# Queuing the leftover work of a decoder layer behind the tile ahead, issuing stores from ScalarE, and transposing new keys into two kinds of PSUM banks

## The chip, the cores and the metric

The kernel runs on one core of a Trainium2 chip. The metric is the device time of one execution in microseconds (us), lower is better.

## What is computed

One inference step of one hybrid decoder layer, for a prompt of 2048 tokens and for 64 new tokens (8 sequences of 8) that look back into a cache of keys and values:

```python
h = rms_norm(x, g_norm)
proj = jnp.einsum('bsd,de->bse', h, w_in)            # 1024 -> 3584 columns
u, va, za, q, k, vb, zb = jnp.split(proj, SPLITS, axis=-1)
...
# mixer A: chunked spatial gating, 4 groups of 128 channels
mixed = jnp.einsum('gts,bnsgc->bntgc', ws, vc) + b_s
a = rms_norm(u * mixed) * jax.nn.silu(z)
...
# mixer B: 8 heads of 64, three dilated windows (128,1), (512,4), (2048,16)
s = jnp.einsum('brnqhd,brnkhd->brnhqk', qb, kb) * SCALE
...
o = jnp.einsum('brnhqk,brnkhd->brnhqd', p, vb) / den
b = combine_by_denominator(outs, lses)
...
h = x + jnp.einsum('bse,ed->bsd', jnp.concatenate([a_out, b], axis=-1), w_out)
gate = jax.nn.sigmoid(jnp.einsum('bsd,de->bse', h, w_ple_gate))
e = rms_norm(jnp.einsum('bsp,pd->bsd', p, w_ple), g_ple)
return h + gate * e
```

The same steps are done for the new tokens, whose attention reads the cached keys and values (2048 rows for each of 8 sequences) beside the new ones.

## The kernel before

The prompt is cut into 16 tiles of 128 rows; the 64 new tokens are a 17th tile of half the height. The input projection has eight chunks of weights, four for mixer A (384 columns) and four for mixer B (512 columns), taken in the order A0, B0, B1, A1, B2, B3, A2, A3. In each chunk the loop runs over the 17 tiles: `gemm` (L473) makes 24 matmuls into a PSUM tile `psg`, for a chunk of A ScalarE and VectorE gate the result (L613 to L617, tanh and multiply, the last reader of the PSUM bank is the multiplication into `agz`), and 4 tiles make one group for the spatial mixing (L648 to L671). The new tokens' rows are split over both halves of the partitions and folded together (`fold`, L483 to L487, with one DMA between).

Between the projection's matmuls a pump lays the dilated attention of the chunks already done. A unit of it is: scores on TensorE (L823, PSUM `pss`), mask and maximum on VectorE (L829), exp on ScalarE (L838), its high half (L841), the low half on VectorE (L842), a transposing DMA on SP's queue (`pT`<-`pc`, L763), the product with the values on TensorE (L869 to L871, PSUM `pso`), and its eviction on ScalarE (`rec`, L875), which a DMA stores to one of the scratch tensors `r1d`, `r2d`, `r3d` (L883). There are 160 such `pc` tiles and 96 such stores. When the three windows of a pair of heads are done, `combine` loads them back (L891), joins them (L901 to L926) and stores the result to `catd` (L928). Four groups of rows are joined for each pair of heads.

The last part takes the tiles one after the other: `p3_cat` loads a row tile of `catd`, splits it into two fp16 halves and transposes them by DMA (`halves_T`, L995 to L998, tile `Tc`), `p3_out` multiplies by `w_out` (gemm2, L1008, 48 matmuls) and adds the residual (L1055), `p3_gate` does the same with `Th`, `p3_ple` with `Tp` (12 matmuls). Its weights are prepared during the last chunk: load (L940), squares (L949), scale and split (L964 on ScalarE, L965 on VectorE). Among these matmuls stands the new tokens' attention, `sample(hp)` for each of the four head pairs: a step for each block of cached keys transposes it on TensorE (L1243, four transposes into PSUM `pst`), copies it to SBUF on ScalarE (`KT`, L1253), and multiplies (L1248); a second part multiplies the keys by the queries on GpSimd (L1263) and sums them on VectorE (L1264).

Each engine's instructions run in the order of its queue. That order is set when the program is built, by a scheduler that sorts by the order of writing and its own reckoning of when each operand is there. `tc.issue_after(ins)` puts the instructions of a block, on the engine of `ins`, behind `ins`. DMAs are issued by the queue of SP throughout, apart from a few small ones on GpSimd.

## Time and profile before

| | before |
|---|---|
| time, median of 3 executions (lowest, highest) | 1474.05 us (1469.55, 1478.37) |
| the profiled execution | 1471.11 us, of which the span 1469.4 us |
| TensorE (PE) busy | 1296.9 us, 88% |
| VectorE (DVE) busy | 999.6 us, 68% |
| ScalarE (ACT) busy | 821.8 us, 56% |
| GpSimd (POOL) busy | 315.7 us, 21% |
| mean granted clock of TensorE | 0.954 |

The span is the time from the first to the last instruction. TensorE is idle for 1469.4 − 1296.9 = 172.5 us of it, and the profile tells for each of these waits which line waited and what ended it. The granted clock is the share of TensorE's full clock that the chip gave in a stretch.

### The profile page before, as it was taken

What the parts mean: (1) busy time and instruction counts of PE and PEld (TensorE: products, weight loads), DVE (VectorE), ACT (ScalarE), POOL (GpSimd) and SP (SyncE); (2) the same over time, 40 slices, a digit from 0 to 9 for tenths busy, and PEclk for the clock granted to TensorE, in tenths of its full rate; (3) what the DMA queues carried; (4) which work ended last, traced back from release to release, by engine and by line L of the source; (5) the groups of instructions that cost most, each with busy time, mean ns of one, the idle gap of its engine ahead of it and who ended that gap; (6) DMA issues with size and microseconds to landing.
All of it is one profiled execution on the core that took longest, in us unless ns stands there. A gap on an engine that the chain in (4) does not pass through costs nothing.

```text
span 1469.4 us, 26262 instructions
## 1 busy us (share of the span) xinstructions
PE 1296.9 (88%) x8600; PEld 674.0 (46%) x8600; DVE 999.6 (68%) x3018; ACT 821.8 (56%) x2269; POOL 315.7 (21%) x279
## 2 busy tenths in 40 slices
PE   4899998998898897899788985569998998999998
PEld 2564454544564554455455653224443443444343
DVE  4675776777777698777778788885455456456364
ACT  5785778966679677687677884553222122123122
POOL 8221001102101111100120025311152143134001
PEclk9899999999999999999999998779999999999999
DMA  5954598799847989978996798976899799989542
GB/s 145 235 132 114 124 173 182 173 222 226 193 112 165 206 188 209 178 185 189 222 213 145 154 247 216 288 173 170 203 210 245 181 203 229 230 184 231 137 88 65
DMA packets 589592, 271.32 MB, mean 185 GB/s; under 512 B 323184, under 2 KB 571056, under 8 KB 589456
## 3 DMA queue, kind: packets, MB, share of 16 engines
q1 hardware_dynamic: 587472, 268.00, 80.7%
q0 software_dynamic: 1984, 1.66, 0.7%
q8 instruction: 67, 1.10, 0.3%
q14 instruction: 69, 0.57, 0.1%
HBM read 136.94 MB, written 55.08 MB: 131 GB/s over the span
## 4 chain that ended last, share of the span: by engine, by line
PE 44%; DMA 23%; DVE 14%; ACT 11%; issue 4%; SPq 3%; POOL 1%; DVEq 0%; ACTq 0%; POOLq 0%
PE psg L473 14%; PE psg L1008 11%; PE pss L1008 10%; DMA pT<-pc 6%; DMA rl<-r2d 2%; DVE sm L829 2%; ACT sm L838 2%; DMA K<-in_cache_k_dram 2%; DMA qB<-qd 2%; DMA wst<-in_w_in_dram 2%; PE pso L1343 2%; DVE pc L842 2%; PE pso L1248 2%; ACT kc L715 1%; DMA rl<-r3d 1%
## 5 line engine op out<-in xcount | busy, mean ns | idle before, releaser
L473 PE MATMUL psg<-wt,xT 128*128 128x512 f16 (+1 forms) x3072 | 640.6, 363 | 31.3 <-DVE agz L617 26.5
L473 PEld LDWEIGHTS <-xT 128*128 128x128 f16 x3072 | 301.7, 100 | 299.7 <-issue 44.3
L193 POOL TENSOR_TENSOR sm<-sm,mhalf 128x1 f32<-128x1 f32 (+5 forms) x115 | 145.6, 1271 | 790.4 <-DVE sm L532 324.6
L838 ACT ACTIVATE sm<-sm,rec 128x256 f32<-128x256 f32 (+1 forms) x384 | 151.7, 459 | 38.9 <-DVE rec L834 35.8
L829 DVE CUSTOM_DVE_ANT_0 sm<-pss,mask,psc 128x256 f32<-128x256 f32 (+1 forms) x384 | 145.1, 419 | 12.2 <-PE pss L823 8.5
L1008 PEld LDWEIGHTS <-Tc 128*128 128x128 f16 x800 | 76.8, 99 | 116.0 <-issue 28.5
L1263 POOL TENSOR_TENSOR K<-K,qB 96x512 f32<-96x512 f32 x64 | 94.1, 1475 | 161.2 <-DMA qB<-qd 62.3
L842 DVE TENSOR_TENSOR pc<-sm,pc 128x512 f16<-128x512 f32 (+1 forms) x160 | 104.2, 653 | 34.1 <-ACT pc L841 32.7
L1008 PEld LDWEIGHTS <-Th 128*128 128x128 f16 x800 | 76.7, 98 | 109.0 <-issue 15.3
L995 ACT ACTIVATE hl<-x,sm 128x1024 f16<-128x1024 f32 (+1 forms) x17 | 19.5, 1148 | 147.3 <-DVE sm L976 132.4
L869 PEld LDWEIGHTS <-pT 128*128 128x128 f16 x600 | 57.1, 98 | 96.1 <-DMA pT<-pc 90.5
L1008 PE MATMUL psg<-w,Th 128*128 128x512 f16 x400 | 95.8, 381 | 5.0 <-DMA Th<-hl 5.0
L841 ACT ACTIVATE pc<-sm 128x512 f16<-128x512 f32 (+1 forms) x160 | 96.0, 603 | 7.2 <-DMA pT<-pc 6.2
L1008 PE MATMUL psg<-w,Tc 128*128 128x512 f16 x400 | 97.0, 386 | 2.8 <-DMA Tc<-hl 2.8
L1264 DVE TENSOR_REDUCE blk<-K 96x8 f32<-96x512 f32 x64 | 43.4, 680 | 79.5 <-POOL K L1263 79.5
L1008 PE MATMUL pss<-w,Tc 128*128 128x512 f16 x400 | 96.0, 382 | 0.0
L1008 PE MATMUL pss<-w,Th 128*128 128x512 f16 x400 | 93.4, 379 | 0.0
L823 PEld LDWEIGHTS <-qk 128*128 128x128 f16 x960 | 74.2, 120 | 29.3 <-issue 5.9
L1100 POOL TENSOR_TENSOR tg<-tg,x 128x1024 f32<-128x1024 f32 (+1 forms) x16 | 37.6, 2348 | 153.9 <-DVE tg L1099 141.8
L869 PE MATMUL pso<-v,pT 128*128 128x65 f16 x248 | 32.2, 201 | 42.4 <-DMA pT<-pc 42.4
L869 PE MATMUL pso<-vt,pT 128*128 128x65 f16 x352 | 43.5, 195 | 28.9 <-DMA pT<-pc 28.8
L715 ACT ACTIVATE kc<-qk 128x512 f16<-128x512 f16 x72 | 58.9, 872 | 13.8 <-DMA qk<-qkd 8.5
(321 smaller groups left out, 2239.5 us busy)
## 6 DMA issues: line engine op xcount, KB each, us to landing
qB<-qd SPq DMA_DIRECT2D x64, 192.0 KB
K<-in_cache_k_dram SPq DMA_DIRECT2D x64, 192.0 KB
V<-in_cache_v_dram SPq DMA_DIRECT2D x64, 192.0 KB
vt<-vscr SPq DMA_DIRECT2D x32, 258.0 KB
K<-in_cache_k_dram SPq DMA_DIRECT2D x32, 256.0 KB
cat<-catd SPq DMA_DIRECT2D x16, 512.0 KB
x<-in_x_prompt_dram SPq DMA_DIRECT2D x16, 512.0 KB
V<-in_cache_v_dram SPq DMA_DIRECT2D x32, 256.0 KB
```

What stands on the lines that cost most here:

```text
L193: nc.gpsimd.tensor_tensor(y, src, mhalf[:p, :n], op=ALU.pow)
L473: last_mm[0] = nc.tensor.matmul(g[:, :ncol], lhsT=l, rhs=r, start=(n == 0), stop=(n == (23 if j < NT else 15)))
L715: nc.scalar.activation(t[:, h], src[:, h], AF.Copy)
L823: nc.tensor.matmul(pss[:, s, h, b * w:(b + 1) * w], lhsT=Q[:, h, qs], rhs=keys(h, k), start=(i == 0 and b == 0), stop=(i == 1 and b == n - 1))
L829: nc.vector.tensor_tensor_reduce(sm4[:, s, h], pss[:, s, h], mk, psc, -3.0e38, op0=ALU.add, op1=ALU.max, accum_out=mx[:, i:i + 1])
L838: nc.scalar.activation(sm4[:, s, h], sm4[:, s, h], AF.Exp, bias=r[:, sl + s, h, HD + 1:HD + 2])
L841: nc.scalar.activation(pc[:, :n], smv, AF.Copy)
L842: nc.vector.tensor_tensor(pc[:, n:2 * n], smv, pc[:, :n], op=ALU.subtract)
L869: nc.tensor.matmul(po[:, q, h, 0:65], lhsT=H, rhs=v[:, vs_, a:a + 65], start=(bi == 0), stop=False)
L1008: last_mm[0] = nc.tensor.matmul(gs[hf], lhsT=o[part][:, kt], rhs=w[:, kt % 2, half, :], start=(n[hf] == 0), stop=(n[hf] == (3 if m == P el ...
L1263: nc.gpsimd.tensor_tensor(K3, K3, qB, op=ALU.mult)
L1264: nc.vector.tensor_reduce(s3[:, b, :, ts_].rearrange("p h t -> p t h"), K3.rearrange("p t (h d) -> p t h d", d=HD), axis=AX.X, op=ALU.add)
```

## The change

It has four parts.

1. A helper `late()` puts a block's instructions behind the last projection matmul on TensorE, and behind the last marked instruction on three other queues: on VectorE the last full tile's gating multiplication (L617, L526) or residual addition (L1055), on ScalarE the last gating tanh (L616, L525, L1096), on SP the last transposing DMA (L763, or the second one of `halves_T`, L998). The blocks are `combine`, every step of the preparation of the last part's weights, and every step of `sample`.
2. ScalarE's queue issues the 96 stores of `rec` (L883), the 14 moves of the fold (L484), and half of the first chunk's eight weight loads (L351): 114 DMAs that SP issued before.
3. The transposes of the new tokens' cached keys go by turns to PSUM tag "o" (two buffers) and "t" (one buffer); before, all went to "t".
4. In the last chunk the new tokens' tile is projected after the eighth tile; before, it came last.

```diff
+    last_on = {}
+    def late():
+        c = ExitStack()
+        for i in [last_mm[0]] + list(last_on.values()):
+            if i is not None:
+                c.enter_context(tc.issue_after(i.ins))
+        return c
...
-                    nc.sync.dma_start(t[:, k2, :ncol].rearrange("p (s c) -> p s c", c=P), src)
+                    (nc.scalar if fast and k2 else nc.sync).dma_start(
+                        t[:, k2, :ncol].rearrange("p (s c) -> p s c", c=P), src)
...
-        nc.sync.dma_start(c[:TS, :n], c[TS:, :n])
+        nc.scalar.dma_start(c[:TS, :n], c[TS:, :n])
...
-        nc.scalar.activation(th[:m], g[:m, 256:384], AF.Tanh, scale=sc[:m, 2:3])
-        nc.vector.scalar_tensor_tensor(G["gz"][:m, q, :], th[:m], 1.0, g[:m, 256:384], op0=ALU.add, op1=ALU.mult)
+        tanh = nc.scalar.activation(th[:m], g[:m, 256:384], AF.Tanh, scale=sc[:m, 2:3])
+        gate = nc.vector.scalar_tensor_tensor(G["gz"][:m, q, :], th[:m], 1.0, g[:m, 256:384], op0=ALU.add, op1=ALU.mult)
+        if m == P:
+            last_on.update(dve=gate, act=tanh)
...
-                nc.sync.dma_start(o["pT"][:, :2 * o["n"] // P, :], o["pc"][:, :2 * o["n"]], transpose=True)
+                last_on["sp"] = nc.sync.dma_start(o["pT"][:, :2 * o["n"] // P, :], o["pc"][:, :2 * o["n"]], transpose=True)
...
-                combine(hp, jg, sc, *got)
+                with late():
+                    combine(hp, jg, sc, *got)
...
-            nc.sync.dma_start(dst[:, s0:s0 + 2], rc)
+            nc.scalar.dma_start(dst[:, s0:s0 + 2], rc)
...
-            nc.vector.scalar_tensor_tensor(h[:m, sl], gs[hf][:m], cm[:m], h[:m, sl], op0=ALU.mult, op1=ALU.add)
+            last_on["dve"] = nc.vector.scalar_tensor_tensor(h[:m, sl], gs[hf][:m], cm[:m], h[:m, sl], op0=ALU.mult, op1=ALU.add)
...
-                pt = pst("t", 1)
+                pt = pst(*(("o", 2) if n % 2 else ("t", 1)))
...
-            yield from sample(hp)
+            steps = sample(hp)
+            while True:
+                with late():
+                    dt = next(steps, None)
...
-        for j in range(NT + 1):
+        for j in range(NT + 1) if ci + 1 < len(order) else [*range(8), NT, *range(8, NT)]:
...
-                    next(nxt, None)
+                    with late():
+                        next(nxt, None)
```

How the change moves instructions is seen at three places. The first is VectorE's queue at the last gating multiplications of the last chunk (L617 before, L629 after; `agz` is their result). Before, one of them stands behind this run, in which `w` is a prepared weight tile (L965), `blk` a sum of the new tokens' scores (L1264) and `gzl` a joined group (L926):

```order
2254 L965 SCALAR_TENSOR_TENSOR w_2247_12774<-w3st_12344,sm_12701,w_2247_12774 128x512
2255 L1264 TENSOR_REDUCE blk<-K_2448_13668 96x4x2
2256 L965 SCALAR_TENSOR_TENSOR w_2247_12774<-w3st_12344,sm_12701,w_2247_12774 128x512
2257 L926 TENSOR_TENSOR gzl_12559<-rl_12553,gzl_12559 128x512
2258 L965 SCALAR_TENSOR_TENSOR w_2250_12809<-w3st_12346,sm_12701,w_2250_12809 128x512
2259 L667 TENSOR_SCALAR sm_12755<-sm_12755,sm_10973 128x4
2260 L965 SCALAR_TENSOR_TENSOR w_2250_12809<-w3st_12346,sm_12701,w_2250_12809 128x512
2261 L965 SCALAR_TENSOR_TENSOR w_2251_12814<-w3st_12348,sm_12701,w_2251_12814 128x512 x2
2262 L624 TENSOR_SCALAR sm_12824<-sm_12543,sm_10973 128x4
2263 L617 SCALAR_TENSOR_TENSOR agz_12545<-th_12821,psg_12784 128x128
```

After, the last full tile's gating multiplication stands among the new tokens' small masks and the last attention unit, ahead of the joining (`rl`, L917 to L936):

```order
2237 L1200 CAST sc_12952<-blk 128x64
2238 L857 TENSOR_TENSOR pc_12405<-sm_12390,pc_12405 128x512
2239 L1201 SCALAR_TENSOR_TENSOR blk<-sc_12952,blk 128x64
2240 L638 TENSOR_SCALAR sm_13191<-sm_12904,sm_10973 128x4
2241 L629 SCALAR_TENSOR_TENSOR agz_12906<-th_13188,psg_13115 128x128
2242 L681 TENSOR_SCALAR sm_13131<-sm_13131,sm_10973 128x4
2243 L1202 TENSOR_SCALAR blk<-blk 128x64
2244 L1206 CAST sc_12952<-blk 128x16
2245 L917 TENSOR_TENSOR sm_12663<-sm_12663,rl_12554 128x8
```

The tiles of `w_out` and of the gate weights (`w` at L980 in the changed kernel) stand behind this point, from row 2270 on, and no sum L1264 stands ahead of them.

The second place is TensorE's queue where the last part begins (`Tc`, the first joined tile). Before, the product of the new tokens' `Tp` with its weights stands directly ahead of it:

```order
12302 L1008 LDWEIGHTS Tp_12991
12303 L1008 MATMUL psg_13216<-w_2132_12170,Tp_12991 128x512
12304 L1008 LDWEIGHTS Tp_12991
12305 L1008 MATMUL psg_13216<-w_2132_12170,Tp_12991 128x512
12306 L1008 LDWEIGHTS Tc_13122
12307 L1008 MATMUL pss_13288<-w_2238_12708,Tc_13122 128x512
```

After, the last attention units' products with the values (L884 to L886, before L869 to L871) stand there, and a sum over partitions of the weights' squares (L283):

```order
12302 L885 LDWEIGHTS pT_12574
12303 L885 MATMUL pso_12576<-vt_12230,pT_12574 128x64
12304 L886 LDWEIGHTS pT_12574
12305 L886 MATMUL pso_12576<-vt_12230,pT_12574 128x65
12306 L283 MATMUL pso_12729<-sm_12632,ones 128x1
12307 L1023 LDWEIGHTS Tc_13180
12308 L1023 MATMUL psg_13274<-w_2245_12740,Tc_13180 128x512
```

Before, the attention's last product stood 137 projection matmuls of the prompt ahead of the end of the projection; after, the last four units' products stand behind all of them.

The third place is the stores of the attention's results. Before, they stand in SP's queue among the transposing DMAs (`pT`<-`pc`):

```order
340 L883 DMA r2d_112<-rec_6647 128x264
341 L763 DMA_TRANSPOSE pT_6985<-pc_6876 128x8x128
342 L763 DMA_TRANSPOSE pT_7188<-pc_7041 128x4x128
343 L556 DMA out_dram<-vo_6822 128x4x128
344 L557 DMA vscr_101<-v_1189_6821 128x4x258
345 L558 DMA zscr_105<-gz_6823 128x4x128
346 L763 DMA_TRANSPOSE pT_7205<-pc_7056 128x8x128
347 L686 DMA vt_7740<-vscr_101 128x1032
348 L883 DMA r2d_112<-rec_6709 128x264
```

After, such a store stands in ScalarE's queue directly behind the eviction (L890) that fills it, ahead of the next unit's exp (L853) and high half (L856):

```order
837 L531 ACTIVATE v_1292_7332<-psg_7529 128x2x64
838 L890 ACTIVATE rec_7062<-pso_7400 128x4x65
839 L898 DMA r1d_109<-rec_7062 128x2x132
840 L853 ACTIVATE sm_7262<-sm_7262,rec_7209 128x128 x2
841 L401 ACTIVATE wt_7646<-wst_6430,sm_7147 128x512 x2
842 L856 ACTIVATE pc_7273<-sm_7262 128x256
```

SP's queue loses 114 DMAs (1187 to 1073 instructions) and ScalarE's gains them.

## Rows read from the trace of the kernel before

**Rows 1.** The page's first part: each engine's busy time, share of the span, instructions.

```profile
PE 1296.9 (88%) x8600; PEld 674.0 (46%) x8600; DVE 999.6 (68%) x3018; ACT 821.8 (56%) x2269; POOL 315.7 (21%) x279
```

**Rows 2.** TensorE's waits: tile and line, what ended them, us in total, times, longest.

```profile
PE pso L869 <- DMA pT<-pc: 71.2, 57, 3.4
PE psg L473 <- DVE agz L617: 26.5, 3, 15.0
PE pst L1243 <- ACT KT L1253: 19.6, 6, 6.6
PE pso L274 <- DVE junk L304: 16.9, 1, 16.9
```

**Rows 3.** Busy time by stretch: PE, PEld, DVE, ACT, POOL; PE's clock; DMA share; GB/s.

```profile
400.00:600.00 200.00, 180.10 (x1448) 102.65 (x1447) 159.66 (x577) 153.36 (x440) 30.10 (x20) 0.96 0.82 177
880.00:940.00 60.00, 33.75 (x189) 18.70 (x190) 50.58 (x98) 25.01 (x77) 27.95 (x20) 0.80 0.95 238
940.00:1000.00 60.00, 43.40 (x180) 18.31 (x179) 53.77 (x139) 35.51 (x87) 13.10 (x11) 0.83 0.85 205
1000.00:1100.00 100.00, 99.51 (x521) 43.27 (x520) 50.92 (x108) 25.44 (x59) 24.98 (x18) 1.00 0.80 195
```

**Rows 4.** Timeline of TensorE, 880 to 945: start, us, line, tiles [wait, its end].

```profile
883.02 12.84 PE L473 MATMUL psg<-wt,xT 128*128 128x384 f16 x78
...
912.13 5.70 PE L473 MATMUL psg<-wt,xT 128*128 128x384 f16 x24 [14.97 <-DVE agz L617]
929.03 0.80 PE L473 MATMUL psg<-wt,xT 128*128 128x384 f16 x2 [11.21 <-DVE agz L617]
...
939.18 2.75 PE L1008 MATMUL pss<-w,Tc 128*128 128x512 f16 x12
```

**Rows 5.** VectorE's groups from 889 to 912 by line: count, busy us, mean ns.

```profile
L965 DVE SCALAR_TENSOR_TENSOR w<-w3st,sm,w 128x512 f16<-128x512 f32 x15 | 11.6, 805 | 0.0
L1264 DVE TENSOR_REDUCE blk<-K 96x8 f32<-96x512 f32 x6 | 4.1, 679 | 1.4 <-POOL K L1263 1.3
...
L617 DVE SCALAR_TENSOR_TENSOR agz<-th,psg 128x128 f32<-128x128 f32 x2 | 0.5, 274 | 0.0
```

**Rows 6.** Timelines of VectorE, SP and ScalarE from a joined group to `Tc`.

```profile
908.28 0.68 DVE L926 TENSOR_TENSOR gzl<-rl,gzl 128x512 f32<-128x512 f32 x1
908.99 1.10 SPq L928 DMA_DIRECT2D catd<-gzl  x1
918.07 0.46 SPq L1031 DMA_DIRECT2D cat<-catd  x1
929.81 1.20 ACT L995 ACTIVATE hl<-cat,sm 128x1024 f16<-128x1024 f32 x1
931.04 2.99 SPq L996 DMA_TRANSPOSE Tc<-hl  x1
...
995.61 0.74 DVE L965 SCALAR_TENSOR_TENSOR w<-w3st,sm,w 128x512 f16<-128x512 f32 x1
```

**Rows 7.** Timelines of TensorE, ScalarE and VectorE at one wait for a copy.

```profile
1124.71 1.12 PE L1243 MATMUL pst<-ident,K 128*128 128x128 f32 x4 [4.83 <-ACT KT L1253]
...
1121.59 1.15 ACT L995 ACTIVATE hl<-x,sm 128x1024 f16<-128x1024 f32 x1 [12.61 <-DVE sm L976]
...
1116.20 0.68 DVE L1264 TENSOR_REDUCE blk<-K 96x8 f32<-96x512 f32 x1 [7.53 <-POOL K L1263]
```

**Rows 8.** SP's queue, its waits: us in total, times, longest.

```profile
SPq L763 <- DVE pc L842: 59.5, 39, 6.0
...
SPq L883 <- ACT rec L875: 21.4, 21, 2.8
```

**Rows 9.** The stores at L883 into one scratch tensor: ns min/median/max, first and last start.

```profile
L883 SPq DMA_DIRECT2D r2d<-rec x32: 319/500/988, 182.5 to 881.6; - x32
```

**Rows 10.** Timelines of SP and ScalarE at the start, the first chunk's weights.

```profile
1.93 6.45 SPq L351 DMA_DIRECT2D wst<-in_w_in_dram  x8
...
11.98 0.61 ACT L367 ACTIVATE junk<-wst,gno 128x384 bf16<-128x384 f32 x1 [4.58 <-DMA wst<-in_w_in_dram]
```

More of the change, by code (lines that the diff above doesn't have):

```diff
@@ L524, in b_evac @@
         th = wk.tile([P, P], F32, name=nm("th"), tag="th", bufs=2)
-        nc.scalar.activation(th[:m], g[:m, 384:512], AF.Tanh, scale=sc[:m, 2:3])
-        nc.vector.scalar_tensor_tensor(G["gz"][:m, q, :], th[:m], 1.0, g[:m, 384:512], op0=ALU.add, op1=ALU.mult)
+        tanh = nc.scalar.activation(th[:m], g[:m, 384:512], AF.Tanh, scale=sc[:m, 2:3])
+        gate = nc.vector.scalar_tensor_tensor(G["gz"][:m, q, :], th[:m], 1.0, g[:m, 384:512], op0=ALU.add, op1=ALU.mult)
+        if m == P:
+            last_on.update(dve=gate, act=tanh)
     def b_norm(G, sc, gch):
@@ L615, in a_evac @@
         th = wk.tile([P, P], F32, name=nm("th"), tag="th", bufs=2)
-        nc.scalar.activation(th[:m], g[:m, 256:384], AF.Tanh, scale=sc[:m, 2:3])
-        nc.vector.scalar_tensor_tensor(G["gz"][:m, q, :], th[:m], 1.0, g[:m, 256:384], op0=ALU.add, op1=ALU.mult)
+        tanh = nc.scalar.activation(th[:m], g[:m, 256:384], AF.Tanh, scale=sc[:m, 2:3])
+        gate = nc.vector.scalar_tensor_tensor(G["gz"][:m, q, :], th[:m], 1.0, g[:m, 256:384], op0=ALU.add, op1=ALU.mult)
+        if m == P:
+            last_on.update(dve=gate, act=tanh)
     def a_norm(G, sc, gch):
@@ L997, in halves_T @@
         nc.vector.scalar_tensor_tensor(lo[:m], t[:m], r[:m], hi[:m], op0=ALU.mult, op1=ALU.subtract)
-        nc.sync.dma_start(dst[1], lo[:m], transpose=True)
+        last_on["sp"] = nc.sync.dma_start(dst[1], lo[:m], transpose=True)
         return o, mx, r
@@ L1095, in p3_gate @@
             sl = slice(hf * 512, hf * 512 + 512)
-            nc.scalar.activation(t[:m, sl], gs[hf][:m], AF.Tanh, scale=cm[:m])
+            last_on["act"] = nc.scalar.activation(t[:m, sl], gs[hf][:m], AF.Tanh, scale=cm[:m])
         dst = yp[j * P:(j + 1) * P] if j < NT else ysm
@@ L1372, in all_samples @@
         for hp in range(4):
-            yield from sample(hp)
+            steps = sample(hp)
+            while True:
+                with late():
+                    dt = next(steps, None)
+                if dt is None:
+                    break
+                yield dt
     ring = dict(cat=[], x=[])
@@ L1474, in tile_hymba_gmlp_dilated_attn_step @@
                 for _ in range(1 if ci else FIRST_PREP[j]):
-                    next(nxt, None)
+                    with late():
+                        next(nxt, None)
             else:
                 for _ in range(LAST_PREP[j]):
-                    if next(nxt, None):
-                        break
+                    with late():
+                        if next(nxt, None):
+                            break
                 if j == 12:
@@ L1541, in tile_hymba_gmlp_dilated_attn_step, with deal @@
     last, cur, samp = None, 0, True
+    def deal():
+        with late():
+            next(nxt, None)
     for k in range(23):
-        pump.later(850.0 * (k + 1), lambda: next(nxt, None))
+        pump.later(850.0 * (k + 1), deal)
     p3_ple(0)
```

## The prediction

> **What bounds the kernel now.** I read the busy times first [rows 1]: TensorE works for 1296.9 us of a span of 1469.4, VectorE for 999.6, ScalarE for 821.8. The change adds and removes no matmul, so its gain can only come out of TensorE's 172.5 idle us, or out of matmuls that ran at a reduced clock. Next come the waits of TensorE [rows 2]. Four entries make 134.2 us of the 172.5: the attention's products wait for the transposed weights `pT` (71.2 us in 57 waits, 1.2 us on the mean), the projection waits for VectorE's gating multiplication to free a PSUM bank (26.5 us in 3 waits), the transposes of the new tokens' keys wait for ScalarE's copy (19.6 us in 6), and the start waits once for 16.9 us. Third come the stretches [rows 3]: in the attention stage (400 to 600 stands for it) TensorE is busy for 180 us in 200, with VectorE at 160 and ScalarE at 153 close below; at the turn from projection to the last part, 880 to 1000, it works for 33.8 + 43.4 = 77.2 us in 120, at a granted clock of 0.80 and 0.83; from 1000 on it is all but full. So the turn is the dear place, and there the order of VectorE's queue decides: TensorE's two long waits of 14.97 and 11.21 us end with a gating multiplication [rows 4], and between two of these stand 15 weight preparations of 805 ns and 6 sums of 679 ns, 15.7 us of VectorE's time, with hardly any idle time in front of them [rows 5].
>
> The sum is made against the profiled execution, 1471.1 us (span 1469.4 and 1.7 outside). The median of the runs shown is 1474.05, so I subtract the same difference from that. About 0.5% (7.4 us) is what a measurement of this kernel can tell from no change.
>
> **A. The start.** SP takes 6.45 us to issue the eight weight loads, and ScalarE waits until 11.98 for one of them [rows 10]. With half of the issues on ScalarE's queue, which has nothing else to do then, the last is issued up to 3.2 us sooner and the next input tile with it. Above: 3.2, and a little more from the tile, 5 us. Below: if the loads are limited by their transfers, nothing, or a loss of 1 because the loads now compete with the first input tile. The wait ends 3.6 us after SP's last issue, so transfers count as much as issues; I take 2. By the Trainium skill, page "DMA: Bandwidth & Descriptors", section "Issuing engines are not separate DMA queues", DMAs of all issuing engines run on the same 16 DMA engines, and spreading them saves only the time to initiate them, usually small; if no issue time lies on the path, this term is 0 and the sum 2 us higher.
>
> **B. The attention stage, up to 880.** 96 stores and the fold's moves go from SP to ScalarE. One costs SP 0.5 us (the median of the 32 into one tensor [rows 9]), so about 110 × 0.45 to 0.5 = 50 to 55 us leave SP, and with the stores goes SP's waiting at its head for `rec`, 21.4 us [rows 8]. This matters where a `pT` transposition stands behind such a store. But SP waits 59.5 us for `pc` itself [rows 8]: most transpositions are late because VectorE is, not because SP is, and that is untouched. On the other side, no row shows a DMA issue on ScalarE. Bounds: nothing, or SP's 0.5 us each, in front of an exp or a high half that lead to the next `pc`. ScalarE is busy for 77% of the stretch [rows 3], so there are some 45 us of 200 free, and some 12 us of issues in each 200 fit. Combine and preparation behind the tile's gating free VectorE for the gates in these chunks, too. If all of SP's relief reached TensorE's waits, 30 us of the 71.2 would go; if all of the issues stood in the path of the 57 waits, 57 × 0.5 = 28 us would come. Between these ends I take a gain of 4: the row it is nearest to is SP's 21.4, of which a fifth lies ahead of a transposition that TensorE waits for.
>
> **C. The turn, 880 to 1000.** The two long waits, 26.2 us, are VectorE's queue order, and this order is what the change moves: the weights' preparation and the sums stand behind the last gate instead of between the gates. What stays between two gates (masks, groups' gating, attention) is work of some 1 to 10 us, an estimate from the new order and durations like those in [rows 5], against 4 us for a tile's 24 matmuls (12.84 / 78 each [rows 4]), so some waits of a few us stay. Also 24 matmuls at 912 took 5.70 us where 24 of the 78 take 3.95: 1.75 us from the clock, which goes with the wait. Up to here: 28 us less before the first `Tc`.
>
> Most of it doesn't arrive. `Tc` needs a joined group, and that chain is serial: from the group's end at 908.28, its store at 908.99, the load of the tile at 918.07, its split at 929.81, the transposition at 931.04, to the first matmul at 939.18 [rows 4, 6]. This is 30.9 us. From the load's issue to the split are 11.7; I put the landing and the statistics at about half of that (an estimate by the store, which took 9.1 from its issue to the load's, and the transposition with 8.1 to the matmul), and the rest, with what stands ahead on SP's queue, at 10 us of places behind other work. 20 are DMAs and the work itself. After the change the joining stands behind the last gate, some 19 us of VectorE's durations (15 with the overlap seen in the rows) before the group is there. So from the last gate to the first `Tc` I count 15 + 20 = 35 us, in which TensorE has only the `Tp` products, four attention units and some transposes, 5 us. The new hole is 30 us where the old ones were 28. What is won is behind it: before, VectorE still summed and prepared until 995.61 [rows 6] and TensorE became full at 1000, 60 us after the first `Tc`. VectorE's remaining work after the last gate is about 70 us either way, but now the last gate itself is early: it follows the projection, which, without its waits, ends at about 883 + 142 matmuls × 0.165 (the 78, 24 and 2 of [rows 4] and 38 behind them) + 5 for the `Tp` products and the mixing → 911 us, plus the attention that now lies among it. That puts the end of the preparation near 911 + 70 = 980 to 990 instead of 996, and sets full TensorE 6 to 16 us earlier. I take 11; bounds: a loss of 5, where the last attention units (their `pT` transpositions are alone on the path, up to 3.4 us each) come in addition, and a gain of 25, where the chain to `Tc` runs at its 20 us from an early group.
>
> **D. The last part from 1000.** The longest waits for `KT` are of the kind in [rows 7]: TensorE waits 4.83 us for a copy that stands on ScalarE behind a split (L995), which waited 12.61 us for statistics on VectorE, which stood behind a sum that waited 7.53 us for GpSimd. A second bank lets TensorE do the next four transposes, 1.12 us, inside the wait, but the multiplication behind them (L1248) needs that same copy. So of 19.6 us I count 6 × 0.6 as hidden. That the sums now stand behind the tile's residual addition could shorten the wait of the split; but in the new order up to six sums still stand ahead of the next one. Loads for the new tokens stand on SP behind a tile's second transposition. Value: a gain of 1; bounds 14 and −8. The fold's move on ScalarE and the halfway tile cost nothing that is on the path: no wait for the fold is among the four long entries of [rows 2], since TensorE works on the next tile meanwhile, and the tile's matmuls are the same ones; without that cover one move's issue and landing, a few us, would be paid once.
>
> Sum: −2 − 4 − 11 − 1 = −18 us, 1453 against the profiled execution, **1456** on the scale of the median.
>
> **The rivals.**
>
> *Given back at the turn.* The hole in front of `Tc` takes all of the gates' waits and VectorE's work ends when it did. For it: the chain of 30.9 us and the joining behind the last gate; against: VectorE was the bound in 889 to 912 without idle time, and its backlog is met sooner. C is then −2, B 0, A −2: −4 us, 1470, no change to be told.
>
> *ScalarE becomes the attention's bottleneck.* The stores stand directly behind the eviction that they store, ahead of the next exp. If each holds ScalarE for SP's 0.5 us, the 57 waits for `pT` grow to about 100 us in all; with half of C (−6) and A (−2): +28 − 8 = +20, 1494. For it: ScalarE's 77% share and its place in a unit between two steps on VectorE. Against: it has free time in every 200 us, and TensorE's work ahead of each product gets longer, so that a delay of 0.5 us is often covered. It decides from about 0.3 us on in each of the 96 (57 × 0.3 = 17, which eats the rest of the sum).
>
> *SP was the cause of the `pT` waits.* Its queue is emptied of 50 us of issues and 21.4 of waits, and 25 of the 71.2 us go: −18 − 21 = −39, 1435. For it: transpositions stand behind stores in SP's order; against: the 59.5 us of waits for `pc`.
>
> **How the numbers follow.** The forecast has 0.45, with its own range of −30 to −8 (1444 to 1466); given back 0.22 (of which 0.03 lie beyond 0.5% faster); ScalarE 0.21; SP the cause 0.12. Faster: 0.45 + 0.12 + 0.03 = 0.60; same 0.19; slower 0.21. The range goes from 1430, which leaves 0.05 of the third rival below it, to 1486, which holds a third of the second one and leaves 0.14 above.
>
> **What would show it.** A: the first projection matmul before 21 us. B: the waits for `pT` near 67 us; 95 and more is the second rival, below 50 the third. C: no wait of over 6 us on `agz`; one of 20 to 30 us in front of the first `Tc`; the last weight preparation before 990 on the time line. D: six or so waits for `KT`, now partly in front of L1248. The prediction is wrong if the first `Tc` comes later than 945 or the attention's last product, now behind the projection, moves the whole turn back.

## The result, and the profile after

The changed kernel takes 1491.22 us (median of 4, 1486.76 to 1501.7) against 1474.07 for the kernel before (median of 4); the ratio is 1.0123, with a 95% interval of 1.0076 to 1.0171. It is slower, by more than what can be told from no change. The profiled execution took 1494.78 us, its span is 1493.0 us.

The busy times on the page of the changed kernel answer to [rows 1]:

```profile
PE 1301.0 (87%) x8600; PEld 673.5 (45%) x8600; DVE 992.4 (66%) x3018; ACT 821.2 (55%) x2269; POOL 311.8 (21%) x279
```

TensorE's idle time is 1493.0 − 1301.0 = 192.0 us, 19.5 more than before, and the same 8600 matmuls are busy for 4.1 us more. TensorE's waits in the changed kernel (line, what ended them, total, times, longest) answer to [rows 2]:

```profile
PE pso L884 <- DMA pT<-pc: 60.9, 61, 3.0
PE psg L1023 <- DMA Tc<-hl: 35.8, 2, 30.6
PE pso L283 <- DVE junk L313: 17.8, 1, 17.8
PE pst L1285 <- DVE blk L1279: 12.2, 3, 5.2
...
PE pso L1258 <- DMA K<-in_cache_k_dram: 8.9, 8, 2.3
PE pst L1285 <- DVE sm L1086: 8.3, 1, 8.3
...
PE psg L483 <- DVE agz L629: 0.5, 1, 0.5
```

The waits for `pT` fell from 71.2 to 60.9 us, those on the gates from 26.5 to 0.5, those on the copies `KT` from 19.6 to none worth a row. New are 35.8 us in front of the joined tiles `Tc`, 20.5 us in front of L1285 (the transposes of the new tokens' sums), and 8.9 us for cached keys.

The stretches of the changed kernel (columns as in [rows 3]) show where the loss lies:

```profile
400.00:600.00 200.00, 183.87 (x1474) 104.86 (x1473) 163.89 (x592) 151.31 (x436) 30.80 (x21) 0.98 0.85 178
...
880.00:940.00 60.00, 22.58 (x147) 12.00 (x145) 43.53 (x120) 41.24 (x116) 8.78 (x11) 0.69 0.84 237
940.00:1000.00 60.00, 48.69 (x201) 21.00 (x201) 50.10 (x116) 25.00 (x52) 14.70 (x11) 0.86 0.77 174
1000.00:1100.00 100.00, 91.79 (x449) 37.00 (x445) 51.41 (x107) 23.88 (x57) 27.28 (x20) 0.98 0.93 218
...
1300.00:1400.00 100.00, 89.19 (x455) 38.60 (x452) 51.07 (x101) 22.91 (x56) 31.24 (x22) 0.97 0.99 220
```

The attention stage is better (183.9 busy us in 200 where there were 180.1). From 1000 on TensorE is no longer full: 449 matmuls in the first 100 us where there were 521. Worked out for the whole span, busy time subtracted from each stretch, TensorE's idle time went from 23.4 to 25.1 us in the first 40, from 85.7 to 75.5 between 40 and 880, from 42.8 to 48.7 at the turn (880 to 1000), and from 20.7 to 42.6 after 1000. The rows behind the last two, first of the kernel before, then of the changed one (the second row ends with the span):

```profile
880.00:1000.00 120.00, 77.15 (x368) 37.01 (x369) 104.35 (x236) 60.52 (x163) 41.05 (x30) 0.82 0.90 222
1000.00:1500.00 500.00, 448.75 (x2241) 191.08 (x2239) 248.15 (x511) 111.35 (x250) 118.17 (x84) 0.98 0.76 172
```

```profile
880.00:1000.00 120.00, 71.27 (x345) 33.00 (x344) 93.64 (x235) 66.24 (x168) 23.49 (x22) 0.77 0.81 206
1000.00:1500.00 500.00, 450.36 (x2186) 187.09 (x2182) 253.61 (x515) 110.60 (x248) 127.03 (x93) 0.97 0.82 185
```

So the stages up to 1000 are together some 2.5 us better, and the last part, which I had put at a gain of 1 us, lost what the change cost.

TensorE's timeline at the turn answers to [rows 4]:

```profile
883.80 3.74 PE L483 MATMUL psg<-wt,xT 128*128 128x384 f16 x22
...
930.60 4.95 PE L1023 MATMUL psg<-w,Tc 128*128 128x512 f16 x16 [30.61 <-DMA Tc<-hl]
```

The projection ends near 888 instead of 938, with no long wait in it; the first `Tc` product starts at 930.60, 8.6 us earlier than before, behind one hole of 30.6 us.

### The profile page after: what moved, and what is told of

The parts are those of the page before. It is cut to its first block, busy times and chain, and to the rows that moved or that the text cites. A ratio compares the mean times of both kernels' runs of the same rounds, so it can differ in the third digit from the quotient of the medians.

```text
span 1493.0 us, 26134 instructions
## 1 busy us (share of the span) xinstructions
PE 1301.0 (87%) x8600; PEld 673.5 (45%) x8600; DVE 992.4 (66%) x3018; ACT 821.2 (55%) x2269; POOL 311.8 (21%) x279
## 4 chain that ended last, share of the span: by engine, by line
PE 40%; DMA 24%; DVE 13%; ACT 10%; SPq 5%; issue 5%; POOL 1%; POOLq 0%; ACTq 0%; DVEq 0%
PE psg L483 16%; PE pss L1023 8%; PE psg L1023 7%; DMA pT<-pc 7%; DMA K<-in_cache_k_dram 4%; PE pso L1358 3%; ACT sm L853 2%; DVE pc L857 2%; DVE sm L844 2%; DMA qB<-qd 2%; DMA rl<-r3d 1%; PE pss L838 1%; ACT kc L729 1%; DMA rl<-r2d 1%; POOL K L1278 1%
## 5 line engine op out<-in xcount | busy, mean ns | idle before, releaser
L483 PE MATMUL psg<-wt,xT 128*128 128x512 f16 (+1 forms) x3072 | 625.0, 357 | 7.1 <-DVE xT L453 2.9
L483 PEld LDWEIGHTS <-xT 128*128 128x128 f16 x3072 | 297.6, 99 | 268.8 <-issue 16.3
L853 ACT ACTIVATE sm<-sm,rec 128x256 f32<-128x256 f32 (+1 forms) x384 | 151.0, 457 | 36.9 <-DVE rec L849 35.5
L1023 PEld LDWEIGHTS <-Tc 128*128 128x128 f16 x800 | 78.6, 101 | 153.5 <-issue 38.5
L1023 PE MATMUL psg<-w,Tc 128*128 128x512 f16 x400 | 100.9, 396 | 35.8 <-DMA Tc<-hl 35.8
L1023 PEld LDWEIGHTS <-Th 128*128 128x128 f16 x800 | 79.0, 101 | 112.4 <-issue 24.0
L1278 POOL TENSOR_TENSOR K<-K,qB 96x512 f32<-96x512 f32 x64 | 87.4, 1369 | 152.9 <-DMA K<-in_cache_k_dram 63.5
L1023 PE MATMUL psg<-w,Th 128*128 128x512 f16 x400 | 102.2, 401 | 6.1 <-DMA Th<-hl 6.1
L856 ACT ACTIVATE pc<-sm 128x512 f16<-128x512 f32 (+1 forms) x160 | 95.3, 602 | 11.4 <-DMA pT<-pc 10.7
L1023 PE MATMUL pss<-w,Tc 128*128 128x512 f16 x400 | 99.8, 386 | 0.0
L1023 PE MATMUL pss<-w,Th 128*128 128x512 f16 x400 | 95.7, 383 | 0.0
L884 PEld LDWEIGHTS <-pT 128*128 128x128 f16 x600 | 56.9, 98 | 85.9 <-DMA pT<-pc 81.0
L1010 ACT ACTIVATE hl<-x,sm 128x1024 f16<-128x1024 f32 (+1 forms) x17 | 19.6, 1151 | 100.5 <-DVE sm L991 89.0
L884 PE MATMUL pso<-vt,pT 128*128 128x65 f16 x352 | 44.0, 197 | 30.6 <-DMA pT<-pc 30.2
L838 PE MATMUL pss<-kc,qk 128*128 128x128 f16 x704 | 62.4, 229 | 6.6 <-DVE sm L844 6.4
## 6 DMA issues: line engine op xcount, KB each, us to landing
K<-in_cache_k_dram SPq DMA_DIRECT2D x64, 192.0 KB
qB<-qd SPq DMA_DIRECT2D x64, 192.0 KB
V<-in_cache_v_dram SPq DMA_DIRECT2D x64, 192.0 KB
```

What stands on the lines that cost most here:

```text
L483: last_mm[0] = nc.tensor.matmul(g[:, :ncol], lhsT=l, rhs=r, start=(n == 0), stop=(n == (23 if j < NT else 15)))
L838: nc.tensor.matmul(pss[:, s, h, b * w:(b + 1) * w], lhsT=Q[:, h, qs], rhs=keys(h, k), start=(i == 0 and b == 0), stop=(i == 1 and b == n - 1))
L853: nc.scalar.activation(sm4[:, s, h], sm4[:, s, h], AF.Exp, bias=r[:, sl + s, h, HD + 1:HD + 2])
L856: nc.scalar.activation(pc[:, :n], smv, AF.Copy)
L884: nc.tensor.matmul(po[:, q, h, 0:65], lhsT=H, rhs=v[:, vs_, a:a + 65], start=(bi == 0), stop=False)
L1023: last_mm[0] = nc.tensor.matmul(gs[hf], lhsT=o[part][:, kt], rhs=w[:, kt % 2, half, :], start=(n[hf] == 0), stop=(n[hf] == (3 if m == P el ...
```

## The experiments

I began with three theories. Theory 1: the change moves the first head pair's key loads from the turn into the last part, which the DMA engines then bound. Theory 2: the banks of tag "o" cost waits. Theory 3: the order of VectorE's sums. A fourth came out of the first four runs. All ratios are against the kernel before, timed on the same chip, with 95% intervals.

**Run 1, the new tokens' steps free.** The loop of `all_samples` is again `yield from sample(hp)`:

```diff
-            steps = sample(hp)
-            while True:
-                with late():
-                    dt = next(steps, None)
...
+            yield from sample(hp)
```

> The changed kernel, but the steps of the new tokens' attention are no longer put behind the tile ahead (the rest of the change stays). Theory 1 (the DMA engines bound the last part, and the change moves the first head pair's cache loads, which lay at the turn from 870 to 946, into it): the loads are back at the turn, the last part wins back some 25 us, the total falls to 1455 to 1470, and the DMA share of 880 to 1000 rises from 0.84 and 0.77 to 0.9 and more. Theory 2 (the banks of tag o for the key transposes are the cause, by waits between the transposes and the products that use the same banks): no change, 1485 to 1497. Theory 3 (the order of VectorE's sums ahead of the residual addition costs the waits): also faster, 1470 to 1480, but without a rise of the DMA share at the turn.

Measured: 1467.94 us, ratio 0.9937 (0.9913 to 0.9961). Theory 2 is out as the cause. Two signs of theory 1 came: the total lies in its range, and the DMA share of 880 to 940 and 940 to 1000 rose to 0.90 and 0.95. But the gain doesn't come out of waiting: TensorE's idle time is 196.4 us, more than in the changed kernel (192.0). What fell is its busy time, from 1301.0 to 1267.5 us, with the same 8600 matmuls. One line stands out in TensorE's groups by shape: first the changed kernel, then run 1 (count of records, busy us, mean ns of one; each fp32 product is recorded as two):

```profile
L1358 PE MATMUL pso<-V,blk 96*32 96x512 f32 x128 | 40.9, 605 | 1.6 <-DMA V<-in_cache_v_dram 1.6
```

```profile
L1358 PE MATMUL pso<-V,blk 96*32 96x512 f32 x128 | 17.1, 605 | 0.0
```

The mean record has 605 ns in both, yet the time in which at least one of the 128 is at work is 40.9 us in one and 17.1 us in the other. The timelines tell why. In the changed kernel, around 1060:

```profile
1054.12 1.06 PE L1358 MATMUL pso<-V,blk 96*32 96x512 f32 x8
...
1059.49 1.05 PE L1358 MATMUL pso<-V,blk 96*32 96x512 f32 x2 [0.96 <-DMA V<-in_cache_v_dram]
1060.47 0.82 PE L1023 MATMUL pss<-w,Tc 128*128 128x512 f16 x3
1061.22 1.04 PE L1358 MATMUL pso<-V,blk 96*32 96x512 f32 x2
1062.20 0.39 PE L1023 MATMUL pss<-w,Tc 128*128 128x512 f16 x1
1062.52 1.04 PE L1358 MATMUL pso<-V,blk 96*32 96x512 f32 x2
```

Four products (8 records) next to each other take 1.06 us; one product alone (2 records) takes 1.04 to 1.05. The four of a group write four different strips of 32 partitions. Side by side they run at once and cost here what one costs; with a main matmul between them each pays the full price. The Trainium skill, page "TensorE: Matmul & The Clock Gate", section "Part 3: Packing small matmuls — row/col tiling", says that matmuls at different tile positions of the array run concurrently; the rows agree, 1.06 us for four against 1.04 for one. Theory 4: the change scatters these groups among the last part's matmuls. The queue's order shows it without a run. Word for word from the changed kernel, TensorE's queue (the weight loads between are left out):

```
13153 L1023 MATMUL pss_14377<-w_2246_12745,Tc_14106 128x512
13154 L1358 MATMUL pso_14191<-V_2552_14131,blk 32x512
13156 L1023 MATMUL pss_14377<-w_2246_12745,Tc_14106 128x512
13158 L1023 MATMUL pss_14377<-w_2246_12745,Tc_14106 128x512
13160 L1023 MATMUL pss_14377<-w_2254_12806,Tc_14106 128x512
13161 L1358 MATMUL pso_14191<-V_2553_14133,blk 32x512
```

The 64 products stand in 26 runs of one to four in the kernel before, in 39 after the change, in 16 in run 1. The busy time at this line follows the number of runs at about 1.05 us each: 27.4, 40.9 and 17.1 us. The row of the kernel before:

```profile
L1343 PE MATMUL pso<-V,blk 96*32 96x512 f32 x128 | 27.4, 605 | 0.0
```

**Run 2, the key transposes in one kind of bank.**

```diff
-                pt = pst(*(("o", 2) if n % 2 else ("t", 1)))
+                pt = pst("t", 1)
```

> The changed kernel with the key transposes all back in tag t. Theory 1: no change, 1484 to 1500. Theory 2: faster by 10 us and more, 1465 to 1480. If the alternation helps by hiding transposes behind the copy: slower by 3 to 10 us, 1494 to 1502.

Measured: 1500.77 us, ratio 1.0152 (1.0114 to 1.0190). The interval overlaps that of the changed kernel, so the total is inconclusive; theory 2 is refuted, since nothing got faster. Two things show what the alternation is good for. With one kind of bank TensorE waits 12.2 us for the copies `KT` again. And the products of the keys (32 strip products, two for each pair of key blocks) are busy for 35.2 us at their line here, for 26.0 in the changed kernel: there eight pairs of them stand side by side, in 24 runs, while here each of the 32 stands alone. First the changed kernel, then this run:

```profile
L1263 PE MATMUL pso<-KT,blk 128*32 128x512 f32 x64 | 26.0, 633 | 0.0
```

```profile
L1263 PE MATMUL pso<-KT,blk 128*32 128x512 f32 x64 | 35.2, 633 | 5.0 <-ACT KT L1268 5.0
```

**Run 3, the loads free on SP.** `late()` leaves SP out for the new tokens' steps:

```diff
-    def late():
+    def late(skip=()):
...
-        for i in [last_mm[0]] + list(last_on.values()):
+        for i in [last_mm[0]] + [v for k, v in last_on.items() if k not in skip]:
...
-                with late():
+                with late(("sp",)):
                     dt = next(steps, None)
```

> The changed kernel, but the steps of the new tokens' attention are put behind the tile ahead on TensorE, VectorE and ScalarE only, not on SP, so that their loads may be issued early while the sums may not. The first head pair has three buffers for these loads, so only the first four or so of its 16 pairs of loads can come early. Theory 1: a part of the gain of the run without any such order, 1478 to 1488. Theory 3: no gain, 1487 to 1497, since the sums stand where they stood. Theory 2: no change.

Measured: 1463.38 us, ratio 0.9894 (0.9852 to 0.9936): all of the loss gone, and more, where theory 1 allowed a part and theory 3 none. Busy time at the values' line is 21.7 us (18 runs), the wait in front of L1285 is 4.5 us instead of 20.5:

```profile
L1358 PE MATMUL pso<-V,blk 96*32 96x512 f32 x128 | 21.7, 605 | 1.4 <-DMA V<-in_cache_v_dram 1.4
```

```profile
PE pst L1285 <- DVE blk L1279: 4.5, 3, 2.6
```

So what hurts is that the loads stand behind a tile's transposition on SP, and it shows in two places: the order is laid out around late loads, and the sums come late. Only the first is seen in the total: TensorE's idle time is 191.7 us, as in the changed kernel (192.0), because waits for the keys' loads (16.4 us) and a longer wait for the first `Tc` (37.7) came in place of those for the sums. Its busy time fell from 1301.0 to 1272.9 us.

**Run 4, this part alone on the kernel before.** The changed kernel with all other parts undone, only this left:

```diff
+            steps = sample(hp)
+            while True:
+                with late():
+                    dt = next(steps, None)
```

> The kernel before with one part of the change alone: the steps of the new tokens' attention behind the tile ahead (key transposes, stores, joining, weights, and the last chunk's order as before). Theory 1: slower than before by 15 to 30 us, 1489 to 1504, with the DMA share of 1000 to 1400 up from 0.885 on the mean to 0.93 and more. Theory 2: no change against before, 1467 to 1481. Theory 3: slower, as theory 1.

Measured: 1476.23 us, ratio 1.0015 (0.9994 to 1.0036). Theories 1 and 3 missed: no loss in total, although the DMA share of 1000 to 1400 did rise as theory 1 had it, from 0.89 to 0.93. The profile shows two things that cancel. The busy time at the values' line is 39.7 us (37 runs), 12.3 more than before, and 12.1 us of waits stand in front of the sums' transposes; but the gates' waits fell from 26.5 to 5.0, and the idle time at the turn is 18.5 us instead of 42.8. So this part alone, with the weights' preparation and the joining left where they stood, takes most of the gates' waits away. The first `Tc` comes at 926.30, with a wait of 4.24 us.

**Run 5, the four products joined.** The changed kernel; the product whose load comes last goes first, and the others are queued behind it:

```diff
-                    for b, v in zip(quad, V3):
+                    first = None
+                    for b, v in list(zip(quad, V3))[::-1]:
...
+                        with tc.issue_after(first.ins) if first is not None else nullcontext():
+                            mm = nc.tensor.matmul(acc[q0:q0 + 32], lhsT=wz[:96, q0:q0 + 32],
...
+                        first = first or mm
```

> The changed kernel; in the second part of the new tokens' values the first of four products (each into its own strip of 32 partitions) is the one whose load comes last, and the other three are queued behind it, so that the four stand next to each other (16 runs of four, where the changed kernel has 39 runs of one to four and the kernel before 26). Theory 4 (four products into four strips run at the same time when they stand next to each other, and the change scatters them between matmuls that fill all strips): TensorE's busy time at this line falls from 40.9 to about 18 us, and the total by 15 to 25, to 1466 to 1476. Theory 1 (cache loads moved into the last part): no change, 1484 to 1498, since all loads stand where they stood.

Measured: 1473.18 us, ratio 1.0002 (0.9984 to 1.0021), 18 us below the changed kernel. Its groups and waits on TensorE:

```profile
L1360 PE MATMUL pso<-V,blk 96*32 96x512 f32 x128 | 18.8, 661 | 8.2 <-DMA V<-in_cache_v_dram 8.2
```

```profile
PE pso L884 <- DMA pT<-pc: 55.6, 59, 3.6
PE psg L1023 <- DMA Tc<-hl: 36.6, 2, 31.4
PE pst L1285 <- DVE blk L1279: 20.0, 4, 7.5
```

The line's busy time fell by 22.1 us, TensorE's by 25.6 in all; 8.2 us of waits for a load of values stand where 1.6 stood, and the span is 20.8 us shorter. All loads stand behind the tile ahead as they did, and the 20 us in front of the sums remain. Theory 4 is right, theories 1 and 3 can't explain this run. The idle time, 196.8 us, stays 24 us above that of the kernel before.

**Run 6, strips in pairs.** Run 1 with the groups as (0, 1, 2, 3) and (4, 5, 6, 7), so that two products of each pair write the same strip:

```diff
+        quad3 = ((0, 1, 2, 3), (4, 5, 6, 7))
...
-            for i, quad in enumerate(quads):
+            for i, quad in enumerate(quad3):
                 V3 = V3s.pop(0)
```

> The run with free steps of the new tokens' attention, where the four products stand next to each other, but the four are now two pairs, each pair into one strip. Theory 4: the busy time at this line doubles from 17 to about 34 us, and the total rises from 1468 by 10 to 17 us. Theory 1: no change against 1468, since the same bytes are loaded.

Measured: 1468.45 us, ratio 0.9977 (0.9958 to 0.9997), against 0.9937 of run 1: slower by 0.40%, give or take 0.31, or 6 us. In its timeline 8 records next to each other now take 1.92 us:

```profile
1045.77 1.92 PE L1359 MATMUL pso<-V,blk 96*32 96x512 f32 x8
```

The busy time at the line rose from 17.1 to 30.7 us with the products still side by side, so being neighbours isn't enough, the strips must differ. (The two products of a pair also add into the same result; this run doesn't part that from the shared strip.) The total rose by less than half of that and by less than I expected; idle time fell by 9 us in the profiled executions. Read the other way round, part of the time that TensorE saves in the last part is waited away.

**Runs 7 and 8, keys late or values late.** Only the steps up to the sums, or only those from the softmax on, behind the tile ahead:

```diff
-            while True:
-                with late():
+            for i in range(99):
+                with late() if i < 12 else nullcontext():
                     dt = next(steps, None)
```

Run 8 has `i >= 12` in the same place.

> The changed kernel, but only the first steps of each head pair's new-token attention (keys, products, sums) are queued behind the tile ahead; softmax and values are free. Its order has 42 runs of one to four products. Theory 4: busy time at this line 40 us and more, total 1486 to 1500. Theory 1: the first head pair's key loads are late, so the same, 1484 to 1498.

> The reverse: the keys' steps are free, softmax and values queued behind the tile ahead. Its order has 21 runs. Theory 4: busy time at this line 21 to 24 us, total 1464 to 1478. Theory 1: key loads are back at the turn, so 1462 to 1475; this run alone doesn't tell the two apart.

Measured: 1486.35 us, ratio 1.0113 (1.0080 to 1.0147) with the keys late; 1462.58 us, 0.9960 (0.9935 to 0.9986) with the values late. Busy time at the values' line: 44.1 us (42 runs) and 24.0 (21 runs). Waits in front of L1285: 11.0 and 2.5 us. The keys' steps are the harmful ones, although the products that get scattered are the values'.

**Run 9, the kernel before with joined products.** The diff of run 5 on the kernel before.

> The kernel before, with nothing of the change, but with the values' products joined into runs of four as in the fifth run. Theory 4: the busy time at this line falls from 27.4 to about 18 us and the total by 5 to 10, to 1462 to 1468 where the kernel before has 1472. If joining helped in the changed kernel only because something else there was disturbed: no change.

Measured: 1470.82 us, ratio 0.9975 (0.9959 to 0.9992). The line's busy time fell from 27.4 to 17.0 us as expected; the total fell by 0.25%, 3.7 us, less than the 5 to 10 expected. TensorE's idle time rose by 9.1 us.

**Run 10, the stores on SP.** Run 5 with

```diff
-            nc.scalar.dma_start(dst[:, s0:s0 + 2], rc)
+            nc.sync.dma_start(dst[:, s0:s0 + 2], rc)
```

> The changed kernel with joined products, and the 96 stores of the attention's results issued by SP again. If the fall of the waits for pT (71.2 to 60.9 us) and of the attention stage's idle time (78.5 to 66.0) comes from the stores: these rise to 68 to 75 and 74 to 80 us, and the total by 6 to 14, from 1473 to 1479 to 1487. If it comes from the work that late() takes out of the queues' way there: no change, 1469 to 1477.

Measured: 1471.46 us, ratio 0.9994 (0.9976 to 1.0013), against 1.0002 (0.9984 to 1.0021) of run 5: the same. Yet the waits for `pT` are 69.4 us where run 5 has 55.6, and the idle time between 200 and 880 is 75.2 where run 5 has 66.0:

```profile
PE pso L884 <- DMA pT<-pc: 69.4, 59, 3.7
```

The stores on ScalarE do give 9 us in the attention stage, as the expectation had it, but the rise of 6 to 14 us in the total that it hung on this didn't come: the 9 us are lost at the turn, where run 5's idle time is 50.8 us and this one's 40.0. TensorE ends the projection at 882.8 in run 5 and at 899.7 here, and the first `Tc` comes at 926.2 and 923.7.

**Runs 11 and 12, what makes the hole before the first joined tile.** Run 5's joined products and run 1's free steps; besides, in run 11 the joining is free, in run 12 the weights' preparation:

```diff
-                with late():
-                    combine(hp, jg, sc, *got)
+                combine(hp, jg, sc, *got)
```

```diff
-                    with late():
-                        next(nxt, None)
+                    next(nxt, None)
```

> The changed kernel with joined products, with the new tokens' steps and the joining of head groups free, only the weights' preparation behind the tile ahead. If the joining behind the last gate makes the wait in front of the first Tc (30.6 us in the changed kernel, 52.4 in the first run): it falls below 25 us, and the total to 1440 to 1458. If not: 1460 to 1470 as the first run.

> The same with the joining behind the tile ahead and the weights' preparation free. If the weights' preparation behind the last gate makes the wait in front of the first Tc: it falls below 25 us and the total to 1440 to 1458; waits on the gates (26.5 us in the kernel before, 0.5 in the changed one) come back by 5 to 20 us. If not: 1460 to 1470.

Measured: run 11 1463.97 us, ratio 0.9931 (0.9903 to 0.9958), as run 1; run 12 1454.78 us, 0.9873 (0.9856 to 0.9889), faster than both kernels. Neither made the hole short. Run 11 waits 45.8 us for `Tc`. In run 12 the wait stands in front of a sum of the weights' squares (L283), which its order puts ahead of the first `Tc`:

```profile
941.79 0.58 PE L283 MATMUL pso<-sm,ones 128*128 128x1 f32 x2 [43.97 <-DVE sm L989]
...
947.91 5.49 PE L1023 MATMUL psg<-w,Tc 128*128 128x512 f16 x16 [4.58 <-DMA Tc<-hl]
```

So that expectation failed, and the gates' waits came back by less than its 5 us, to 4.2. Run 12's gain over run 1 lies mostly behind the hole: 317 matmuls done between 880 and 1000 where run 1 has 244, and 53.3 us idle there where it has 70.9. Behind its first `Tc` run 1 waits 4.0 us more for `Tc` and 5.9 for `Th`, run 12 only 1.6 for `Th`, and the granted clock of 950 to 1000 is 0.98 in run 12, 0.85 in run 1. That the weights, ready earlier, are what lets TensorE go on is likely but not shown: none of these waits ends with a weight.

Run 11 adds one thing on the attention stage. Its stores stand on ScalarE, yet the waits for `pT` are 68.9 us and the idle time between 200 and 880 is 74.2, as in run 10:

```profile
PE pso L883 <- DMA pT<-pc: 68.9, 57, 3.8
```

So the gain there needs both, the stores on ScalarE and the joining out of the way. And again it is worth nothing in the total: run 11's projection ends 16 us after run 1's (899.1 and 883.5), and the times are the same.

## Why the prediction was wrong

Forecast was 1456, with a range of 1430 to 1486 and 0.60 for faster; it came out at 1491, slower.

**A, the start (−2).** Missed. The idle time of the first 40 us went from 23.4 to 25.1; TensorE's first sum waits 17.8 us instead of 16.9. Over all profiles there is nothing to tell: 23.9 to 25.1 in the eleven kernels with the loads on two queues, 23.4 to 25.2 in the three without. The issue was not on the path: the last load was issued at 4.8 us instead of 8.4, but ScalarE's last wait for one of these tiles ended at 16.1 instead of 15.2. By the rule of the Trainium skill that the prediction weighed (page "DMA: Bandwidth & Descriptors", section "Issuing engines are not separate DMA queues") the term was 0, and the rows are nearer to that.

**B, the attention stage (−4).** Right in sign, too small: the waits for `pT` fell by 10.3 us, idle time between 40 and 880 by 10.1. Run 10 shows that without the stores 9 of it are lost, run 11 that without the late joining 8 are: the two don't add up, both are needed. The rival in which ScalarE becomes the bottleneck didn't occur; an issue took 0.33 to 0.38 us there (medians of the three tensors), where 0.3 in the path of each had been put as enough to eat the gain.

**C, the turn (−11).** Half right. The gates' waits went (0.5 us left), the hole of some 30 us in front of `Tc` came as worked out (30.6), the first `Tc` at 930.60, and the last weight tile (L980) starts at 979.3 instead of 995.6. But TensorE didn't become full with it, and idle time at the turn is 5.9 us more, with B's and C's gains arriving there as waiting. Runs 10 and 11 show that a gain ahead of the turn is waited away at it. This step held for the hole and failed in its size. Of the two kinds of work between the gates, run 4 moves only the new tokens' steps and not the weights, and has 5.0 us of gates' waits left; so moving the weights wasn't needed for most of it.

**D, the last part (−1, bounds −14 and +8).** This is the step that failed. I costed the copies' waits and the fold. Of the copies' waits I counted 3.6 us as hidden; all 19.6 went, and run 2 puts 12.2 of them down to the second kind of bank. What I did not cost is what `late()` does to the new tokens' steps. Two terms were missing. First, "the change adds and removes no matmul, so its gain can only come out of" idle time or clock: that sentence is wrong here, since the busy time of the same products depends on their neighbours. The values' products went from 27.4 to 40.9 us (+13.5) by 13 more runs; runs 1, 3, 5 and 8 undo this in four ways, and run 5 changes only the order of these products. The alternating banks gave 9.9 us back at the keys' products (35.9 before, 26.0 after), which I didn't foresee either. Second, the sums: 20.5 us of new waits in front of L1285, in a last part whose idle time rose from 20.7 to 42.6 us. "Loads for the new tokens stand on SP behind a tile's second transposition" was in the text with no price. Run 3, which frees only these loads, has 4.5 us in front of L1285.

The two terms are not equally well shown. Runs 1, 3, 5 and 8 all win back the loss, and in all four it is TensorE's busy time that fell, from 1301.0 to between 1267.5 and 1275.4 us; the idle time stayed at 191.7 to 196.8, where the changed kernel has 192.0 and the kernel before 172.5. So the scattered products are shown to cost some 18 us in total (run 5). That the waits in front of the sums cost anything in total is not shown: where they fell, others came in their place, at the first `Tc` and at the keys' loads, which wait 8.9 us in the changed kernel and 15.4 and 16.4 in the faster runs 1 and 3. No run took the idle time of the last part away by itself.

Of the rivals, the time of the second (1494) was nearly met by coincidence, since its mechanism was wrong: the waits for `pT` fell. The forecast of where the change would give back (the turn) was partly right; that the last part would lose more than all of it was not among the cases.

The prediction's clock term (1.75 us at the turn) holds: the last 22 projection products take 3.74 us, 0.17 each, where 24 took 5.70 behind the wait. The projection's matmuls are busy for 625.0 us in all where they were 640.6, but 10.8 of this lies in the chunks of mixer B, for which nothing was forecast, and run 9, which leaves these as they were, has 5.4 less there, too. What the clock gave back it took elsewhere: behind the new hole 16 products at 930.60 take 4.95 us, and the last part's products with `Tc` and `Th` (L1023) are busy for 398.6 us in all where they were 382.2. Most of that comes later: of the eight stretches of 50 us from 1000 to 1400, six have a granted clock of 0.92 to 0.97 in the changed kernel, three one of 0.93 to 0.97 before. That these products are also interrupted more often by others may have a part in it; the runs don't part the two.

What stays open: how to shorten the way from the last gate to the first `Tc`. It takes 38 us in the changed kernel and 34 to 57 in runs 1 to 3, 5 to 8, 11 and 12; it was shorter only where the last gate came late, at 910 us in run 10 (14 us) and at 922 in run 4 (4 us). Freeing the joining or the weights alone didn't shorten it, and it was not tried to free both. In the changed kernel the trace names its pieces, from the last gate at 892.5:

```profile
910.20 0.68 DVE L941 TENSOR_TENSOR gzl<-rl,gzl 128x512 f32<-128x512 f32 x1
914.17 0.50 SPq L1046 DMA_DIRECT2D cat<-catd  x1
923.25 0.63 ACT L964 ACTIVATE junk<-w3st 128x512 bf16<-128x512 f32 x1 [4.59 <-DMA w3st<-in_w_ple_gate_dram]
925.76 1.13 ACT L1010 ACTIVATE hl<-cat,sm 128x1024 f16<-128x1024 f32 x1
926.92 1.24 SPq L1011 DMA_TRANSPOSE Tc<-hl  x1
```

The joined group is ready 18 us after the gate, and ten weight tiles (7 us) stand among its steps on VectorE. The tile's statistics are there at 920.5, but its split stands on ScalarE behind squares of gate weights that waited for their load until 923.25, some 5 us. So weights stand in the way on two engines there. But run 12, which frees the weights, has the group ready 2 us after its last gate, at 915.9, and is late on SP instead: store, load and first transposition are issued at 920.0, 925.0 and 941.6, among loads of the cache.

## What to carry to other kernels

Before a change that only reorders a queue, count in the new order how often matmuls that share the array (different strips of 32) stand next to each other; four side by side cost here what one costs alone, and in this order, laid out around late loads, they were pulled apart. Where that happens, put the one whose data comes last first and queue the others behind it. When work is put behind the tile ahead, price its loads too: here a load that was late on the queue moved the products that the order lays out around it. When the time changes, look whether idle or busy time changed before explaining it by a wait. And a gain in a stage is worth only what the next serial chain lets through: 9 us of the attention stage were lost in front of the first joined tile.

## What the runs showed of the hardware

Four fp32 products of 96 rows into 32 columns by 512, into four strips, take 1.06 us side by side (runs 1 and 9 and the changed kernel), two into each of two strips 1.92 us (run 6), and one alone 1.04 us. Issuing one of the 96 stores took ScalarE's queue 0.33 to 0.38 us (medians of the three tensors), SP's 0.43 to 0.50 before. The busy time of ScalarE (821.8 us before, 821.2 after) can't tell of this cost, since it doesn't count the issuing of DMAs; what tells is that the waits for `pT` didn't grow, 71.2 us before and 60.9 after.
